# Two transformer layers on one core: later column sums in layer 1's projection stage, transposes moved in layer 0's expert loop

## The chip, the cores and the metric

The kernel runs on one core of a Trainium2 chip. The core has five engines that each work through their own queue in order: TensorE (PE in the profile, its weight loads PEld), VectorE (DVE), ScalarE (ACT), GpSimd (POOL) and SyncE (SP), which here only starts transfers. Engines wait for each other by semaphores. The metric is the device time of one execution in microseconds (us).

## The reference

Two layers work on 1024 latent tokens and 256 context tokens of width 1024. Layer 0 mixes by a short convolution and latent attention, layer 1 by windowed attention; each layer ends in a mixture of 16 experts in which each expert picks its tokens (128 latent and, in layer 0, 32 context tokens). What matters here:

```
aff = softmax(h @ router_w);  g, idx = top_k(aff.T, cap)       # every expert picks its tokens
xg  = h[idx]
hid = silu(xg @ w_gate) * (xg @ w_up)
out = zeros.at[idx].add((hid @ w_down) * g)
mod = silu(c) @ mod_w[layer] + mod_b[layer]                    # six rows of 1024: shift, scale, gate, twice
p   = modulate(rms_norm(x), shift, scale) @ w_qkv              # layer 1's projection, 10 tiles of 128 tokens
```

All arithmetic is float32. A large product is made of three matmuls on high and low parts: an operand is split by a cast on ACT (`wh`, `xh`, `hh`) and a subtraction on DVE (`wl`, `xl`, `hl`).

## The kernel before

**Layer 0's routing and its first expert.** `mixer_out` ends the mixer: it projects tiles of 128 tokens, and ranks the tokens for the experts. For the two context tiles, `OutTile.soft` (line 1290) makes the softmax of the router: two DVE operations, an exponential on ACT, a reciprocal and a product on DVE. Then `table(AF.Silu)` loads ACT's table for the experts. `moe` opens with `prep(0)`: the gathered tokens of expert 0 are transposed on PE and split into `xh` and `xl`; after that one piece of weights is converted, and `route_ctx` picks the context tokens.

**One expert of layer 0** (`expert`, line 1747). Its work on PE stands in program order (`manual_schedule` of PE and POOL); the order on ACT and DVE is laid down when the program is built, by a planner that runs the program in a model and gives each engine what is ready, the earlier in the program first. The order on PE is: `products(0, 0)` and `(0, 1)` (gate and up, first half of the columns), `ctx_products`, `products(1, 0)`, `turn(0)` and `ctx_turn(0)` (transposes of the hidden values, of latent and context tokens), `products(1, 1)`, `ctx_products`, `prep(e + 1)` (eight transposes of the next expert's tokens `xg`), after experts 3, 7 and 11 `prep_ctx` (eight transposes of the next four experts' context tokens `cx`), then the down products, steps `k` = 0 to 7 of six matmuls each, with `turn(1)` and `ctx_turn(1)` ahead of step 2, and last the context's down product `pcd`. All these transposes write the two PSUM buffers of tag B in turn, and a buffer is free again when ACT and DVE have read it: after `prep` that is the cast to `xh` and the subtraction to `xl`, after `ctx_turn` one ACT copy to `chT`. Steps 4 to 7 read `hh[1]` and `hl[1]`, which come from `turn(1)`. The weights have four buffers of `wh` and `wl`; each pair of down steps sets one free, and ACT then casts a piece of the next expert into it.

**Layer 1's projection** (`layer1_mixer`, line 1926) takes the ten tiles in turn, in program order on all queues. Between the products of the tiles it makes four of the six modulation rows that are needed later (`Row`, line 329): a row is four loads of 1 MB of `mod_w` by SP, four uses on DVE (each two multiply-adds of 128 x 1024 into an accumulator) and one `sum`: four small matmuls (`pm`) that add the accumulator over the partitions, one addition on DVE, one store by POOL. `modulations` (line 380) hands out these units one at a time, at most three in a tile, and loads `ahead` pieces ahead; here `ahead` is 1. All four rows share one accumulator, `lent`, borrowed from one of the rings of weight buffers. The sum follows its row's fourth use in the list, and PE takes it in program order between the tile's products.

Of the kernel before, what the change touches and what calls it, by code (L numbers as in the profile page):

```python
# [9 lines left out]
F32 = mybir.dt.float32  # L10
# [5 lines left out]
AF = mybir.ActivationFunctionType  # L16
# [5 lines left out]
D = 1024  # L22
# [14 lines left out]
ROWS_NEXT = [(1, r, (0,)) for r in (3, 4, 2, 5)]  # L37
E = 16
# [59 lines left out]
def hybrid_block_kernel(ctx, tc, A, out, dbg=None, upto=99):  # L98
# [42 lines left out]
    def table(f, src=ones):  # L141

        act.activation(warm, src, f, scale=0.0)

    rp = ctx.enter_context(sbuf("route"))
# [231 lines left out]
        def tile(self, shape, dtype, tag, **_):  # L377
            return self.tiles[tag]

    def modulations(parts, rows, ahead):  # L380

        a, b = [[u for x in xs for u in x.units()] for xs in (parts, rows)]
        todo = sorted([((i + 0.5) / len(x), i, u) for x in (a, b) for i, u in enumerate(x)], key=lambda t: t[0])
        todo = [u for _, _, u in todo]
        loads = [load for load, _ in todo if load]
        n = 0
        for load in loads[:ahead]:
            load()
        for load, use in todo:
            yield  # L390
            use()
            if load:
                n += 1
                for more in loads[n + ahead - 1:n + ahead]:
                    more()
# [793 lines left out]
    class OutTile:  # L1189
# [100 lines left out]
        def soft(self):  # L1290

            a = self.o.aff[self.s][:, self.i, :]
            m, d = [self.wp.tile([128, 1], F32, tag=t, bufs=2, name=t) for t in ("rm", "rd")]
            dve.scalar_tensor_tensor(a, self.lg, self.o.rr[self.s][:, self.i:self.i + 1], router[self.o.l, self.s][1],
                                     op0=ALU.mult, op1=ALU.add)
            dve.tensor_reduce(m, a, axis=AX.X, op=ALU.max, negate=True)
            act.activation(a, a, AF.Exp, bias=m, accum_out=d)
            dve.reciprocal(d, d)
            dve.tensor_scalar(a, a, d, None, op0=ALU.mult)

    def mixer_out(l, w_out, res_x, res_c, h2x_, acc_x_, routed, W):
        with sbuf("ow", side="right" if l else None) as wp, psum("owp", A=(4, 1), B=(2, 1), C=(2, 1)), tc.manual_schedule(engines=QUEUES):
# [161 lines left out]
            if l == 0:  # L1464
                W.convert(1)
                W.load(2)
                for y in tiles[8:]:
                    y.norm()
                o.scale(1)
                for y in tiles[8:]:  # L1470
                    y.mul()
                    y.add()
                    y.store()
                for y in tiles[8:]:
                    y.soft()
                routed[1] = o.aff[1]
                table(AF.Silu)
        if f"xm{l}" in dbg:
            if l == 0:
                pool.dma_start(dbg["xm0"][:NC], acc_c.rearrange("(t j) n -> t (j n)", j=4))  # L1480
# [212 lines left out]
    def moe(l, h2x_, acc_x_, routed, W, gates2, extra, last, early=None, then=None, finish=None, lent=[]):  # L1693
        gi, gv, xgs = {}, {}, {}
        XG, XH, HH, YO = CFG[l]
        with sbuf("moe") as mp, psum("mop", A=(4, 1), B=(2, 1), C=(2, 1)):
# [11 lines left out]
            def prep(e):  # L1708
                xg = xgs.pop(e)
                xh = mp.tile([128, 8, 128], F32R, tag="xh", bufs=XH, name="xh")  # L1710
                xl = mp.tile([128, 8, 128], F32R, tag="xl", bufs=XH, name="xl")
                for b, p in enumerate(transposes8(xg)):
                    bs = slice(b * 4, b * 4 + 4)
                    hilo(xh[:, bs, :], xl[:, bs, :], p.rearrange("p (k t) -> p k t", t=128))
                return xh, xl
# [7 lines left out]
            def prep_ctx(cx):  # L1723
                cT = mp.tile([128, 8, 128], F32, tag="cT", bufs=1, name="cT")
                for b, p in enumerate(transposes8(cx)):
                    act.copy(cT[:, b * 4:b * 4 + 4, :], p.rearrange("p (k t) -> p k t", t=128))
                return cT
# [8 lines left out]
            with tc.manual_schedule(engines=QUEUES):  # L1736
                look_up(0)
                gather(0)
                look_up(1)
                gather(1)  # L1740
                for e in range(2, 3 + 2 * l):
                    look_up(e)
                xT = prep(0)
                if l == 0:
                    W.convert(1)
                    cgi, cgv, cgg = route_ctx(mp, routed[1])
            def expert(e, xT, cT):

                look_up(e + (5 if l else 3))
# [33 lines left out]
                def turn(n):  # L1783

                    (p,) = transposes8(sil[n], 4)
                    hh.append(mp.tile([128, 4, 128], F32R, tag="hh", bufs=HH, name="hh"))
                    hl.append(mp.tile([128, 4, 128], F32R, tag="hl", bufs=HH, name="hl"))
                    hilo(hh[n], hl[n], p.rearrange("p (k t) -> p k t", t=128))
# [39 lines left out]
                    turn(1)  # L1828
                elif e:
                    ctx_products()  # L1830
                xT = prep(e + 1) if e + 1 < E else None
                if l == 0 and not e:
                    cT = prep_ctx(cx)
                    ctx_products()
                    ctx_turn(0)
                cT_ = cT
                if l == 0 and e % 4 == 3 and e + 1 < E:
                    cT_ = prep_ctx(cx)
                if e == E - 1:
                    if l == 0:  # L1840
                        turn(1)
# [5 lines left out]
                for k in range(8):  # L1847
                    if k % 2 == 0:
                        wd.append(W.get())
                    if k == 2 and l == 0:  # L1850
                        turn(1)
                        ctx_turn(1)
                    w = wd[k // 2]
                    for n in range(2):
                        ns = slice(n * 512, (n + 1) * 512)
                        pe.matmul(pd[n], hh[k // 4][:, k % 4], w[2][:, k % 2, ns], start=k == 0, stop=False)  # L1856
                        pe.matmul(pd[n], hh[k // 4][:, k % 4], w[1][:, k % 2, ns], start=False, stop=False)  # L1857
                    for n in range(2):
                        ns = slice(n * 512, (n + 1) * 512)
                        pe.matmul(pd[n], hl[k // 4][:, k % 4], w[1][:, k % 2, ns], start=False, stop=k == 7)  # L1860
# [65 lines left out]
    def layer1_mixer(st1, last, load_qkv, w_qkv, cols, x_first):  # L1926
        with sbuf("l1w") as wp, psum("l1p", A=(4, 1), B=(2, 1), C=(2, 1)):
# [118 lines left out]
            with tc.manual_schedule(engines=QUEUES):  # L2046
                x, y = tiles[:2]
                for z in tiles[:4]:
                    z.load()
                x.table()  # L2050
                w_hi(1)
                x.P()
                x.add()
                x.sq()
                y.P()
                w_hi(2)
                w_lo(dve)
                x.norm()
                w_lo(dve)
                while len(w_qkv) < 8:  # L2060
                    load_qkv()
                x.T()
                x.parts()
                w_hi(1)
                w_lo(dve)
                w_lo(pool)
                y.add()
                y.sq()
                w_hi(2)
                w_lo(dve)  # L2070
                w_lo(pool)
                y.norm()
                w_hi(2)
                w_lo(dve)
                w_lo(pool)
                lender = next(p for p, _ in ring.raws if p is not raw0)
                ring.less(lender)
                lent = Lent(lender.tile([128, 2, D], F32, tag="raw", bufs=2, name="lent"))
                rest = modulations([], [Row(l, r, ss, lent, "B") for l, r, ss in ROWS_NEXT], 1)
                for j in range(TT):  # L2080
                    x = tiles[j]
                    x1_, x2 = tiles[j + 1:j + 2], tiles[j + 2:j + 3]

                    def turn():
                        for y in x1_:
                            y.T()
                            y.parts()

                    for y in x1_:
                        y.table()  # L2090
                    for y in tiles[j + 4:j + 5]:
                        y.load()
                    if j == 0:
                        x.M(range(6), 2, 0, 1)
                        turn()
                        x.M(range(6, 8), 2, 0, 1)
                    for y in x2:
                        y.P()
                    if j not in (0, 1, 8):
                        turn()  # L2100
                    if j:
                        x.M(range(8), 2)
                        tiles[j - 1].q(1)
                    for y in x2:
                        y.add()
                        y.sq()
                        y.norm()
                    if j:
                        steps(rest, 1)
                    x.kv()  # L2110
                    if j > 1:
                        steps(rest, 1 if j < TT - 1 else 99)
                    if not x.s:
                        if j:
                            x.M(range(8), 0)
                        if j in (1, 8):
                            turn()
                        x.q(0)
                        if j:
                            steps(rest, 1)  # L2120
                            x.M(range(8), 1)
# [418 lines left out]
```

## Time and profile before

| | us |
|---|---|
| median of 3 runs | 2937.06 (2931.83 to 2937.67) |
| the profiled execution | 2937.01 |
| its span in the trace | 2935.2 |
| PE busy | 2693.3 (92%) |
| DVE busy | 2202.3 (75%) |
| ACT busy | 1618.6 (55%) |

A view of waits names who waited for whom, with total, times and longest. In a timeline a row is one instruction or several merged ones: start, duration, engine, line, operation, what it writes and reads, shapes, count, and in brackets how long the engine had been idle before it and what ended that. A view of windows gives the busy time of each engine in a stretch.

### The profile page before, as it was taken

Reading aid. Unit: us, or ns where it says so; the run is one execution under the profiler, and the core shown is the slowest. Engines: PE = TensorE matmul, PEld = TensorE weight load, DVE = VectorE, ACT = ScalarE, POOL = GpSimd, SP = SyncE. Lnnn points to the kernel's source line nnn. Section 1 sums busy time; section 2 is a strip of 40 time slices with the busy share of each in tenths; the row PEclk is TensorE's granted clock in tenths of the full one; section 3 lists DMA queues with packets and bytes.
Section 4 is the critical chain, followed back from the end, with each engine's and each line's share of the span. In section 5 each row is a group of like instructions: output and inputs, shape, how many; then the busy total and the mean of one; then the engine's idle time right before and its main releaser. Section 6 shows DMA issues by size and latency. Waiting matters only on the chain.

```text
span 2935.2 us, 43443 instructions
## 1 busy us (share of the span) xinstructions
PE 2693.3 (92%) x16939; PEld 2162.9 (74%) x16939; DVE 2202.3 (75%) x3425; ACT 1618.6 (55%) x2443; POOL 450.1 (15%) x294
## 2 busy tenths in 40 slices
PE   6999899999879999999999887799988599999996
PEld 5989899987657677677677665678867488877775
DVE  4775799986776666666666565799966688888886
ACT  4101578773245555555555532589943377776664
POOL 2100000000012110202111200232200522221103
PEclk8999999999989999999999998799999799999998
DMA  6552000027468787788787554311157699999993
GB/s 265 192 177 91 4 10 10 9 75 240 161 236 308 266 284 281 273 297 287 269 282 245 180 186 149 128 37 30 30 160 260 199 377 384 383 381 373 365 354 135
DMA packets 277198, 614.44 MB, mean 209 GB/s; under 512 B 25320, under 2 KB 73184, under 8 KB 274944
## 3 DMA queue, kind: packets, MB, share of 16 engines
q1 hardware_dynamic: 261840, 567.91, 53.8%
q0 software_dynamic: 15008, 43.62, 5.6%
q8 instruction: 133, 2.18, 0.3%
q14 instruction: 73, 0.60, 0.1%
q10 hardware_dynamic: 144, 0.13, 0.0%
HBM read 549.94 MB, written 61.67 MB: 208 GB/s over the span
## 4 chain that ended last, share of the span: by engine, by line
PE 68%; DVE 10%; ACT 4%; issue 4%; DMA 2%; POOL 1%; SPq 0%; DVEq 0%; ACTq 0%; POOLq 0%
PE pw L1223 6%; PE pg L1771 4%; PE pu L1773 4%; PE pu L1774 4%; PE pu L1776 4%; PE pg L1772 4%; PE pg L1775 4%; PE pd L1860 3%; PE pd L1856 3%; PE pd L1857 3%; PE po L979 3%; PE po L2267 2%; PE ppt L953 2%; PE pcg L1796 2%; PE ptr L407 2%
## 5 line engine op out<-in xcount | busy, mean ns | idle before, releaser
L1098 DVE TENSOR_TENSOR wl<-raw,wh 128x2048 fp32r<-128x2048 f32 x385 | 868.1, 2282 | 295.4 <-ACT wh L1097 295.4
L1097 ACT CAST wh<-raw 128x2048 fp32r<-128x2048 f32 (+1 forms) x392 | 733.8, 1902 | 336.8 <-PE pg L1775 218.8
L1865 POOL DMA_INDIRECT acc_x<-yo,gp x30 | 116.0, 3867 | 699.7 <-DVE yo L1864 658.8
L1771 PE MATMUL pg<-wl,xh 128*128 128x512 f32 x512 | 209.6, 409 | 4.5 <-ACT xh L164 4.5
L1773 PE MATMUL pu<-wl,xh 128*128 128x512 f32 x512 | 204.5, 399 | 6.0 <-DVE wl L1098 6.0
L1772 PE MATMUL pg<-wh,xh 128*128 128x512 f32 x512 | 203.8, 398 | 0.0
L1774 PE MATMUL pu<-wh,xh 128*128 128x512 f32 x512 | 203.1, 397 | 0.0
L1776 PE MATMUL pu<-wh,xl 128*128 128x512 f32 x512 | 203.1, 397 | 0.0
L1775 PE MATMUL pg<-wh,xl 128*128 128x512 f32 x512 | 203.0, 396 | 0.0
L1856 PE MATMUL pd<-wl,hh 128*128 128x512 f32 x480 | 195.6, 407 | 1.6 <-ACT csl L1802 1.6
L1857 PE MATMUL pd<-wh,hh 128*128 128x512 f32 x480 | 194.7, 406 | 0.0
L1860 PE MATMUL pd<-wh,hl 128*128 128x512 f32 x480 | 153.4, 401 | 1.0 <-DVE hl L165 1.0
L168 PE MATMUL pc<-hT,wh 128*128 128x256 f32 x480 | 140.2, 292 | 6.8 <-DVE h L481 5.0
L170 PE MATMUL pc<-hT,wl 128*128 128x256 f32 x480 | 137.6, 287 | 4.8 <-DVE wl L501 4.8
L169 PE MATMUL pc<-hT,wh 128*128 128x256 f32 x480 | 136.5, 284 | 0.0
L1771 PEld LDWEIGHTS pg<-wl,xh 128*128 128x128 f32 x512 | 96.7, 189 | 41.3 <-issue 17.1
L1773 PEld LDWEIGHTS pu<-wl,xh 128*128 128x128 f32 x512 | 96.6, 189 | 33.8 <-DVE wl L1098 11.5
L1780 ACT ACTIVATE sil<-pg 128x512 f32<-128x512 f32 x64 | 38.3, 598 | 143.8 <-PE pg L1775 143.8
L1796 PE MATMUL pcg<-raw,cT 128*32 128x256 f32 x2048 | 116.9, 381 | 0.1
L960 ACT CAST pt<-ppt 128x512 fp32r<-128x512 f32 (+1 forms) x192 | 95.0, 515 | 39.2 <-PE ppt L953 37.1
L964 DVE TENSOR_TENSOR pt<-ppt,pt 128x512 fp32r<-128x512 f32 (+1 forms) x192 | 110.6, 593 | 7.7 <-ACT pt L960 5.2
L1775 PEld LDWEIGHTS pg<-wh,xl 128*128 128x128 f32 x512 | 96.6, 189 | 23.2
(459 smaller groups left out, 6607.2 us busy)
## 6 DMA issues: line engine op xcount, KB each, us to landing
raw<-in_exp_w_gate_dram SPq DMA_DIRECT2D x128, 1024.0 KB
raw<-in_exp_w_up_dram SPq DMA_DIRECT2D x128, 1024.0 KB
raw<-in_exp_w_down_dram SPq DMA_DIRECT2D x128, 1024.0 KB
raw<-in_mod_w_dram SPq DMA_DIRECT2D x48, 1024.0 KB
yT<-yTd SPq DMA_DIRECT2D x17, 512.0 KB
acc_x<-xn SPq DMA_DIRECT2D x16, 512.0 KB
h2x<-h SPq DMA_DIRECT2D x16, 512.0 KB
raw<-in_w_in_dram SPq DMA_DIRECT2D x8, 768.0 KB
```

The lines of the kernel that those rows point to most:

```text
L1097: act.copy(wh[:, cs], raw[:, cs])
L1098: (eng or dve).tensor_sub(wl[:, cs], raw[:, cs], wh[:, cs].bitcast(F32))
L1223: pe.matmul(self.pp[n], a[:, k], b[k // 2][:, k % 2, ns], start=(k == 0 and i == 0), stop=(k == 7 and i == 2))
L1771: pe.matmul(pg, xh[:, k], gl[:, j], start=k == 0, stop=False)
L1772: pe.matmul(pg, xh[:, k], gh[:, j], start=False, stop=False)
L1773: pe.matmul(pu, xh[:, k], ul[:, j], start=k == 0, stop=False)
L1774: pe.matmul(pu, xh[:, k], uh[:, j], start=False, stop=False)
L1775: pe.matmul(pg, xl[:, k], gh[:, j], start=False, stop=k == 7)
L1776: pe.matmul(pu, xl[:, k], uh[:, j], start=False, stop=k == 7)
L1856: pe.matmul(pd[n], hh[k // 4][:, k % 4], w[2][:, k % 2, ns], start=k == 0, stop=False)
L1857: pe.matmul(pd[n], hh[k // 4][:, k % 4], w[1][:, k % 2, ns], start=False, stop=False)
L1860: pe.matmul(pd[n], hl[k // 4][:, k % 4], w[1][:, k % 2, ns], start=False, stop=k == 7)
```

## The change

Three edits. (1) `modulations` gets a parameter `late`: each sum is moved that many units down the list. Layer 1's rows are now loaded three pieces ahead, use two accumulators in turn, and are summed two units late. (2) The context tiles' softmax is cut in two: the two DVE operations stay in `mixer_out`, the exponential, the reciprocal, the product and the load of ACT's table are called in `moe` just before `route_ctx`, behind `prep(0)` and one conversion. (3) In layer 0's experts 1 to 14, `prep(e + 1)` moves from ahead of the down products to ahead of their step 4, `prep_ctx` to ahead of step 6, `ctx_turn(1)` to ahead of step 4, and `turn(1)` to ahead of step 0 (the two turns also in expert 0).

```diff
-    def modulations(parts, rows, ahead):
+    def modulations(parts, rows, ahead, late=0):
         a, b = [[u for x in xs for u in x.units()] for xs in (parts, rows)]
+        for i in reversed([i for i, (load, _) in enumerate(b) if not load] if late else []):
+            b.insert(i + late, b.pop(i))
...
-            m, d = [self.wp.tile([128, 1], F32, tag=t, bufs=2, name=t) for t in ("rm", "rd")]
+            m, d = [(rp if self.s else self.wp).tile([128, 1], F32, tag=t, bufs=2, name=t) for t in ("rm", "rd")]
...
+            self.s_ = a, m, d
+            if not self.s:
+                self.soft_rest()
+
+        def soft_rest(self):
+            a, m, d = self.s_
             act.activation(a, a, AF.Exp, bias=m, accum_out=d)
...
-                routed[1] = o.aff[1]
-                table(AF.Silu)
+
+                def soft():
+                    for y in tiles[8:]:
+                        y.soft_rest()
+                    table(AF.Silu)
+                    return o.aff[1]
+
+                routed[1] = soft
...
-                    cgi, cgv, cgg = route_ctx(mp, routed[1])
+                    cgi, cgv, cgg = route_ctx(mp, routed[1]())
...
-                xT = prep(e + 1) if e + 1 < E else None
+                xT = prep(e + 1) if (l or not e) and e + 1 < E else None
...
-                if l == 0 and e % 4 == 3 and e + 1 < E:
-                    cT_ = prep_ctx(cx)
...
-                    if k == 2 and l == 0:
+                    if l == 0 and k == 0:
                         turn(1)
+                    if l == 0 and k == 4:
                         ctx_turn(1)
+                        if e:
+                            xT = prep(e + 1)
+                    if l == 0 and k == 6 and e % 4 == 3:
+                        cT_ = prep_ctx(cx)
...
-                lent = Lent(lender.tile([128, 2, D], F32, tag="raw", bufs=2, name="lent"))
-                rest = modulations([], [Row(l, r, ss, lent, "B") for l, r, ss in ROWS_NEXT], 1)
+                lent = [Lent(lender.tile([128, 2, D], F32, tag="raw", bufs=2, name="lent")) for _ in range(2)]
+                rest = modulations([], [Row(l, r, ss, lent[i % 2], "B") for i, (l, r, ss) in enumerate(ROWS_NEXT)], 3, 2)
```

## Rows read from the trace of the kernel before

**Rows 1.** The page, part 1: busy time, share, instructions of each engine.
```profile
PE 2693.3 (92%) x16939; PEld 2162.9 (74%) x16939; DVE 2202.3 (75%) x3425; ACT 1618.6 (55%) x2443; POOL 450.1 (15%) x294
```

**Rows 2.** Windows: stretch, length, busy time of the engines, clock, DMA; layer 1's projection.
```profile
1700.00:1800.00 100.00, 81.62 (x345) 62.45 (x344) 65.53 (x127) 27.59 (x56) 2.80 (x5) 0.88 0.55 187
...
1694.20:1708.90 14.70, 13.80 (x64) 10.96 (x62) 12.42 (x24) 5.78 (x13) 0.54 (x1) 1.00 0.90 315
```

**Rows 3.** Waits of PE and of DVE, 1620 to 1845: total, times, longest.
```profile
PE pm L361 <- DVE lent L353: 27.8, 4, 9.5
...
DVE lent L353 <- DMA raw<-in_mod_w_dram: 12.9, 7, 3.9
```

**Rows 4.** Timeline of PE around the sums of layer 1's rows.
```profile
1743.72 1.92 PE L361 MATMUL pm<-lent,ones 128*32 128x512 f32 x4 [9.50 <-DVE lent L353]
1745.57 0.80 PE L168 MATMUL pqkv<-wl,hh 128*128 128x512 f32 x1
...
1749.98 0.39 PE L169 MATMUL pqkv<-wh,hh 128*128 128x512 f32 x1
1750.21 0.40 PE L170 MATMUL pqkv<-wh,hl 128*128 128x512 f32 x1
...
1822.07 1.92 PE L361 MATMUL pm<-lent,ones 128*32 128x512 f32 x4 [9.39 <-DVE lent L353]
```

**Rows 5.** Timeline of DVE: the last two uses ahead of the last sum.
```profile
1815.68 2.61 DVE L353 SCALAR_TENSOR_TENSOR lent<-raw,csil,lent 128x1024 f32<-128x1024 f32 x2 [3.28 <-DMA raw<-in_mod_w_dram]
1819.41 2.61 DVE L353 SCALAR_TENSOR_TENSOR lent<-raw,csil,lent 128x1024 f32<-128x1024 f32 x2 [1.13 <-DMA raw<-in_mod_w_dram]
```

**Rows 6.** Windows, one for each of experts 1 to 14, and their sum.
```profile
1126.09:1174.14 48.05, 47.75 (x360) 34.57 (x364) 33.09 (x24) 27.16 (x24) 6.98 (x4) 1.00 0.82 287
1174.14:1228.08 53.94, 50.50 (x368) 36.77 (x372) 33.09 (x24) 28.33 (x26) 9.89 (x5) 0.97 0.74 266
...
sum 691.57, PE 678.00 PEld 492.02 DVE 464.21 ACT 383.90 POOL 110.53; mean PE 48.43 PEld 35.14 DVE 33.16 ACT 27.42 POOL 7.90
```

**Rows 7.** Timeline of PE: an ordinary expert, then one with `prep_ctx`.
```profile
1266.66 0.66 PE L407 MATMUL ptr<-ident,sil 128*128 128x128 f32 x4 [0.30 <-DVE xl L165]
...
1406.63 1.09 PE L407 MATMUL ptr<-ident,xg 128*128 128x128 f32 x8
1410.81 1.25 PE L407 MATMUL ptr<-ident,cx 128*128 128x128 f32 x8 [3.08 <-DVE xl L165]
...
1414.36 0.63 PE L1856 MATMUL pd<-wl,hh 128*128 128x512 f32 x1
```

**Rows 8.** Timeline of ACT in two experts.
```profile
1362.50 1.90 ACT L1097 CAST wh<-raw 128x2048 fp32r<-128x2048 f32 x1 [1.71 <-PE pd L1860]
...
1364.78 0.27 ACT L1812 COPY chT<-pct 128x128 f32<-128x128 f32 x1
...
1407.50 0.38 ACT L1802 ACTIVATE csl<-pcg 64x256 f32<-64x256 f32 x1
```

**Rows 9.** Waits of PE's weight loads, 880 to 1590.
```profile
PEld pd L1860 <- DVE hl L165: 4.9, 14, 0.8
```

**Rows 10.** Timeline of PE after two short waits in expert 0.
```profile
840.10 0.50 PE L1773 MATMUL pu<-wl,xh 128*128 128x512 f32 x1 [1.37 <-DVE wl L1098]
...
865.48 0.50 PE L1856 MATMUL pd<-wl,hh 128*128 128x512 f32 x1 [1.59 <-ACT csl L1802]
...
867.45 0.63 PE L1857 MATMUL pd<-wh,hh 128*128 128x512 f32 x1
```

**Rows 11.** Timelines of PE and of ACT around `prep(0)`.
```profile
818.63 1.97 PE L407 MATMUL ptr<-ident,xg 128*128 128x128 f32 x8 [11.27 <-DMA xg<-h2x,gp]
825.14 0.76 PE L1771 MATMUL pg<-wl,xh 128*128 128x512 f32 x1 [4.54 <-ACT xh L164]
...
823.02 1.28 ACT L143 ACT_TABLE_LOAD   x1
...
824.43 1.05 ACT L164 CAST xh<-ptr 128x512 fp32r<-128x512 f32 x2
```

## The prediction

> **What bounds the kernel now.** I read the page first. Part 1 shows PE busy in 92% of the span [rows 1], so a gain has to come out of PE's remaining 8%, or out of stretches in which PE runs at the lower of its two clock levels. The windows then say where that is: in the hundred microseconds of layer 1's projection PE is busy 81.62 at a mean granted clock of 0.88 [rows 2], while an ordinary expert of layer 0 has PE busy 47.75 of 48.05 at full clock [rows 6]. The waits of PE name the cause in the projection: one group, the small matmuls `pm` behind DVE's accumulation, 27.8 us in four waits [rows 3]. In the experts the reader is to see that three of the fourteen last 53.94 or a little more instead of 48.05 [rows 6], and in the timeline what is in them: a wait of 3.08 for `xl` ahead of the transposes of `cx` [rows 7]. Ahead of expert 0 PE stands for 4.54 because `xh` comes late [rows 11]. These are the three places that the change touches.
>
> **Part 1, layer 1's rows.** Before: PE meets a sum in program order and waits until DVE has made the row's fourth use. DVE is late for two reasons: it waited 12.9 us for pieces of `mod_w` that were loaded only one ahead [rows 3], and it is nearly full, 12.42 of 14.70 us in a tile with three uses [rows 2]. Afterwards PE goes on at half pace: behind the wait of 9.50 the ten matmuls from 1745.57 to 1749.98 take 4.41, where the pace is 0.23 each (1749.98 to 1750.21), so 2.1 too long, and `pm` takes 1.92 where an undisturbed one has about 1.05 by the same factor; together 2.9 [rows 4]. [...]
>
> After: in the list of units (four uses and a sum for each row) sums 1 to 3 stand two uses later, which is most of a tile (72 products of 0.23, some 17 us), against a longest wait of 9.5. They find their accumulators ready, and the second buffer lets the next row start without them. The loads are three ahead, and there are three buffers, so a load now waits on SP for the use that frees its buffer; behind it in SP's queue stand stores that wait for later DVE work anyway, so that costs nothing. POOL's stores of the rows move with the sums; the tile loads queued behind them are needed more than a tile later. The number of uses, sums, loads and stores stays.
>
> The fourth sum can't move: the list ends behind it, so it still follows its use directly. Of its wait of 9.39 [rows 4] the two waits for transfers, 3.28 and 1.13, go [rows 5], and one use of 2.5 goes too, since a sum takes the place of a use in the tile before. 2.5 stays, plus a slow stretch behind it.
>
> Sum: 27.8 - 2.5 = 25.3 of waits, plus the slow stretches behind the second and third wait, 2.9 and (a shorter wait) about 2: 30 us. What is late next is DVE: three uses in a tile take 84% of PE's time as shown, so tiles with a sum and two uses have room. Bounds: 34 if even the last wait goes with its clock; 24 if DVE lags by its 2 us of slack at each of the four sums.
>
> **Part 2, the context softmax.** Before, the eight transposes end at 820.60 and the cast to `xh` begins at 824.43, because ACT has two exponentials and the table load (1.28, from 823.02) first [rows 11]. After, the casts come first: the first half is transposed by about 819.6, so `xh` is there near 820.2 instead of 825.0, and PE could start 4.5 sooner. The same 3 us of ACT work now stand between the third and the fourth conversion of weights, so the second pair of weights may be late by 1 to 1.5, inside what was gained. The context's exponentials move from before 823.0 to about 824 (the casts to 821.2, a conversion of 1.9), and the list that hangs on them is needed only when expert 0's four products are through, over 20 us later. I take 3.5 less. Bounds: 4.5 (the whole wait), and 1.5 more than before (the fourth conversion late and nothing gained, because the gather of the context's tokens ends the first expert's wait).
>
> **Part 3, the experts.** Fourteen experts take 691.57 [rows 6]. What goes: the 0.30 ahead of `turn(1)` [rows 7] in eleven of them, 3.3; the waits of the down products for `hl`, 4.9 over all [rows 9], since `turn(1)` now comes four steps (5.5 us) ahead of its first reader; and in the three long ones the 3.08 and the slow stretch behind it. Such an expert is 53.94 - 48.05 = 5.89 longer; 1.0 of it are the transposes of `cx` (1410.81 to the next), 2.78 the longer wait, the remaining 2.1 the lower clock (0.63 where 0.39 is usual, until past 1414.36 [rows 7]). So 3 x (3.08 + 2.1) = 15.5. Sum 23.7.
>
> What comes: (a) The down products start about 0.3 sooner after `ctx_products`, because a `turn` is half as long as `prep`; their second PSUM buffer is free only when ACT has made `csl`, at 1407.88 where the products now would want it at 1407.6 [rows 7, 8]: 0.25 each, 3.5 in all.
>
> (b) A new wait. The second half of `prep` needs the buffer that `ctx_turn(1)` has just filled, so PE waits for ACT's copy to `chT`. Step 3 has just set weight buffers free at that moment, and ACT is idle. The rows show what ACT's fixed order makes of this one place earlier: as soon as a down step releases a buffer it starts the cast (1362.50), and `chT`, ready a moment later, follows behind it (1364.78) [rows 8]. So I expect the cast first: 1.81 until the next instruction, and 0.27 for `chT`, 2.15 with the signals, while PE has only six of eight transposes' worth of work (about 0.7 of the 0.85 that eight take). The wait is 1.45, fourteen times: 20.3. Queued behind it on PE are all the rest of the expert; nothing hides it. From below it costs 0 (the copy goes ahead of the cast), from above two casts, 3.3.
>
> (c) `prep_ctx` at step 6 needs the buffers of `prep`, read by two casts of 0.5 [rows 11] and two subtractions like them, in the 2.8 us of steps 4 and 5: ready just in time, 0. The next expert's `xh` and `xl` have steps 4 to 7, 5.5 us, and `pcd`: 0. `xh` no longer waits for the last product.
>
> Sum: -23.7 + 3.5 + 20.3 = 0. The three long experts lose what the eleven others pay. Bounds: 20 less (no new wait), and more than before if the clock falls (rivals).
>
> Whether a wait of 1.45 lowers the clock: the rows have both. After 1.37 the next matmul is at full pace, after 1.59 matmuls take 0.63 [rows 10]; after 3.08 they did all three times [rows 7]. I take no fall, as after the row nearest to 1.45. [...]
>
> **Sum.** 2937.0 (the profiled execution, span 2935.2 and 1.8 around it; the median of the runs is 2937.06, the same) - 30 - 3.5 + 0 = 2903.
>
> **Rivals.**
> A. No new wait in the experts: `chT` is put ahead of the cast. For it: of things ready together ACT takes the earlier in the program, and `chT` is that. Against it: [rows 8]. 2903 - 20 = 2883.
> B. The clock falls after each of the fourteen new waits, at the price seen after 3.08, 2.1 each, 29 in all: 2932. For it: [rows 10], 1.59. Against it: 1.37 in the same rows.
> C. The change doesn't do in layer 1 what it says: the sums find another wait, since DVE's own work, not the loads, made it late. Half of the 30 comes back: 2918. Against it: two units' distance is more than any wait.
> D. Slower: in the experts the clock, once lowered at step 4, stays so through the rest of the down products. 24 matmuls at 0.43 instead of 0.23 are 4.8; fourteen times 67, so 2970. It decides from 34 / 14 = 2.4 us lost behind each wait, only a little above B's 2.1. Against it: after the 3.08 the slow stretch cost 2.1, not 4.8.
>
> **Chances.** Forecast 0.50, A 0.22, B 0.10, C 0.12, D 0.06. The time is the forecast's. The range 2880 to 2930 holds the forecast with the bounds of parts 1 and 2, A, C, and half of B; outside are D and B's upper half. A measurement of this kernel can tell about 0.2% (6 us) from no change: faster 0.89 (forecast, A, C, half of B), same 0.05 (the other half), slower 0.06 (D).
>
> **What would show it.** Part 1: waits of PE for `lent` fall from 27.8 to a few us in one wait, and the projection's clock stands near 1. Part 2: the cast to `xh` ahead of the table load. Part 3: in ordinary experts a wait ahead of `prep`'s second four transposes, released by `chT`, and windows near 49 us; in A they are near 47.7; in B the clock is below 1 in all of them. Wrong it would be if the ordinary experts lasted over 51, or if `pm` still waited for 10 us or more.

## The result, and the profile after

The changed kernel takes 2898.95 us (median of 4 runs, 2897.56 to 2900.43), the kernel before beside it 2934.56. The ratio is 0.9878, with a 95% interval of 0.9861 to 0.9896, so 30 to 41 us less; the forecast was 2903. One execution of a later kernel, turn_at_3_shift, took 5315 us where its five others took 2888, and its ratio leaves that one out. The profiled execution took 2898.11, its span 2896.3, which is 38.9 less than the span of before.

Layer 1's projection first. The windows, in the columns of [rows 2], are 100 us in the middle of it:

```profile
1664.00:1764.00 100.00, 98.40 (x449) 78.36 (x448) 77.83 (x160) 39.72 (x82) 3.31 (x6) 1.00 0.73 253
```

PE is busy 98.40 of 100 at a clock of 1.00, where [rows 2] had 81.62 at 0.88. The waits of PE have one line left of the four waits in [rows 3]:

```profile
PE pm L361 <- DVE lent L353: 2.0, 1, 2.0
```

The timeline of PE shows the first and the last of the four sums (the second, at 1740.88, and the third, at 1778.06, look like the first); they answer to [rows 4]:

```profile
1707.45 1.05 PE L361 MATMUL pm<-lent,ones 128*32 128x512 f32 x4
...
1786.88 1.05 PE L361 MATMUL pm<-lent,ones 128*32 128x512 f32 x4 [2.02 <-DVE lent L353]
1787.87 0.50 PE L168 MATMUL pqkv<-wl,hh 128*128 128x512 f32 x1
```

All four take 1.05, none 1.92: the granted clock is 1.00 at each of them. Only the last waits, 2.02, and the products behind it are at full pace.

Ahead of expert 0, PE and then ACT, to be read against [rows 11]:

```profile
816.39 1.97 PE L410 MATMUL ptr<-ident,xg 128*128 128x128 f32 x8 [11.34 <-DMA xg<-h2x,gp]
818.27 0.77 PE L1786 MATMUL pg<-wl,xh 128*128 128x512 f32 x1
...
827.07 0.51 PE L1788 MATMUL pu<-wl,xh 128*128 128x512 f32 x1 [1.21 <-DVE wl L1101]
...
840.72 0.24 PE L1547 MATMUL pidx<-ident,cidf 16*32 16x16 f32 x5 [2.49 <-DVE cidf L1540]
```

```profile
817.54 0.59 ACT L164 CAST xh<-ptr 128x512 fp32r<-128x512 f32 x1 [15.49 <-PE ptr L410]
...
820.69 0.31 ACT L1306 ACTIVATE raff<-raff,rm 128x16 f32<-128x16 f32 x1
...
821.39 1.28 ACT L143 ACT_TABLE_LOAD   x1
```

The casts to `xh` come first now and the first product follows the transposes at once; the wait of 4.54 is gone, and 1.21 for the second pair of weights stands in its place. The 1.37 for weights of [rows 10] is gone too, but PE now waits 2.49 for `cidf`, the list of context tokens that hangs on the moved softmax. In the kernel before PE came to that list without a wait:

```profile
844.72 0.26 PE L1532 MATMUL pidx<-ident,cidf 16*32 16x16 f32 x7
```

The experts in windows (an ordinary one, one with `prep_ctx`, the sum of fourteen), then the new wait on PE and on ACT; they answer to [rows 6 to 8]:

```profile
1119.87:1169.05 49.18, 47.69 (x358) 34.59 (x357) 33.12 (x24) 27.27 (x24) 6.97 (x4) 1.00 0.80 281
1169.05:1219.09 50.04, 48.58 (x366) 35.44 (x365) 33.98 (x24) 28.25 (x26) 9.87 (x5) 1.00 0.81 287
...
sum 691.19, PE 670.46 PEld 486.92 DVE 464.56 ACT 384.94 POOL 108.84; mean PE 47.89 PEld 34.78 DVE 33.18 ACT 27.50 POOL 7.77
```

```profile
1155.30 0.50 PE L1874 MATMUL pd<-wl,hh 128*128 128x512 f32 x1 [0.18 <-ACT csl L1817]
...
1160.90 0.66 PE L410 MATMUL ptr<-ident,xg 128*128 128x128 f32 x4
1162.86 0.65 PE L410 MATMUL ptr<-ident,xg 128*128 128x128 f32 x4 [1.31 <-ACT chT L1827]
1163.27 0.48 PE L1874 MATMUL pd<-wl,hh 128*128 128x512 f32 x1
```

```profile
1160.74 1.91 ACT L1100 CAST wh<-raw 128x2048 fp32r<-128x2048 f32 x1 [0.89 <-PE pd L1878]
1162.55 0.26 ACT L1827 COPY chT<-pct 128x128 f32<-128x128 f32 x1
```

The cast is ahead of the copy to `chT`, PE waits 1.31 for it, and the clock stays at 1.00 in all fourteen. The long experts are shorter by 3.9 us (the first by 4.9), the ordinary ones longer by 1.1, and the sum is what it was. The waits of PE from 860 to 1600 put it in one line:

```profile
PE ptr L410 <- ACT chT L1827: 18.2, 14, 1.3
```

So far the forecast holds. But the terms measured in this profile (30.4 in the projection, 3.5 ahead of expert 0, 0.4 in the experts) leave 4.6 of the 38.9 over: 2.2 ahead of `prep(0)` and 2.4 behind the projection. Both are within what executions of like code differ by: copies_3 and copies_of_chT below, which are the kernel after in both places, reach `prep(0)` at 819.0 and 816.5 (after 816.4, before 818.6) and take 1086.7 and 1088.9 behind the projection (after 1089.5, before 1091.9). And whether a term comes from the edit that it was put down to, one pair of profiles can't say.

### The profile page after: what moved, and what is told of

Read it like the earlier page. It is cut to its first block, busy times and chain, and to the rows that moved or that the text cites. A ratio compares the mean times of both kernels' runs of the same rounds, so it can differ in the third digit from the quotient of the medians.

```text
span 2896.3 us, 43462 instructions
## 1 busy us (share of the span) xinstructions
PE 2677.9 (92%) x16939; PEld 2152.5 (74%) x16939; DVE 2200.8 (76%) x3425; ACT 1620.5 (56%) x2443; POOL 449.8 (16%) x294
## 4 chain that ended last, share of the span: by engine, by line
PE 71%; DVE 7%; ACT 6%; issue 2%; DMA 1%; POOL 1%; SPq 0%; DVEq 0%; ACTq 0%; POOLq 0%
PE pw L1226 6%; PE pg L1786 4%; PE pu L1788 4%; PE pu L1789 4%; PE pu L1791 4%; PE pd L1878 4%; PE pd L1874 4%; PE pg L1790 4%; PE pg L1787 4%; PE pd L1875 4%; ACT wh L1100 3%; PE po L982 3%; PE po L2285 2%; PE ppt L956 2%; PE ptr L410 2%
```

## The experiments

All were timed in five rounds beside the kernel before (median 2935.85 to 2937.04 in the three groups; the kernel after as above). Stages of each profiled execution, us: from the transposes of `prep(0)` to expert 0's first `pcd`; the fourteen experts; from there to the load of `ks` that ends the projection; what follows up to the end. The 816 to 821 us ahead of `prep(0)` are not in the table.

| kernel | median | ratio (95%) | prep(0) | experts | projection | behind it |
|---|---|---|---|---|---|---|
| before | 2937 | 1 | 60.1 | 691.6 | 273.0 | 1091.9 |
| after | 2899.0 | 0.9878 (0.9861 to 0.9896) | 56.6 | 691.2 | 242.6 | 1089.5 |
| rows_only | 2904.4 | 0.9881 (0.9866 to 0.9896) | 60.4 | 691.6 | 244.2 | 1093.1 |
| loads_only | 2927.8 | 0.9972 (0.9962 to 0.9982) | 60.3 | 691.5 | 265.5 | 1089.3 |
| late_only | 2915.9 | 0.9930 (0.9913 to 0.9947) | 60.2 | 691.7 | 252.3 | 1092.4 |
| soft_only | 2928.8 | 0.9966 (0.9954 to 0.9979) | 57.1 | 688.2 | 277.0 | 1086.1 |
| shift_128 | 2926.1 | 0.9965 (0.9954 to 0.9975) | 59.2 | 684.3 | 274.1 | 1087.1 |
| experts_only | 2937.8 | 0.9998 (0.9989 to 1.0007) | 60.1 | 693.7 | 276.3 | 1091.2 |
| no_soft | 2907.4 | 0.9902 (0.9887 to 0.9916) | 58.8 | 693.7 | 245.9 | 1088.9 |
| no_soft_shift | 2903.9 | 0.9892 (0.9877 to 0.9906) | 59.8 | 691.2 | 242.4 | 1089.5 |
| turn_at_3 | 2882.2 | 0.9811 (0.9795 to 0.9826) | 56.8 | 675.8 | 241.2 | 1089.5 |
| turn_at_3_shift | 2888.2 | 0.9838 (0.9825 to 0.9850) | 56.8 | 678.3 | 243.1 | 1089.5 |
| copies_3 | 2898.7 | 0.9874 (0.9857 to 0.9891) | 56.6 | 691.2 | 242.7 | 1086.7 |
| copies_of_chT | 2969.0 | 1.0114 (1.0100 to 1.0129) | 56.6 | 762.9 | 242.9 | 1088.9 |

### Layer 1's rows: all of edit 1, its loads, its place

rows_only is the kernel before with edit 1 as it stands; the other two take it apart:

```diff
 rows_only:   Row(..., lent[i % 2], "B") ..., ahead 3, late 2
 loads_only:  Row(..., lent[i % 2], "B") ..., ahead 3, late 0
 late_only:   Row(..., lent[i % 2], "B") ..., ahead 1, late 2
```

> The kernel before with edit 1 alone (layer 1's rows). Theory (the three parts add up, and part 1 is 30 us of PE waiting for sums and of the lower clock behind them): 30 us less than before, some 2905; PE waits for `lent` once, about 2 us, ahead of the last sum; the projection's stretch is some 30 shorter, everything ahead of it is as before. Rival (part of those 30 us is had only because the stretches ahead were changed too, so that the pieces of `mod_w` come at other moments): 15 to 20 less, with a second wait for `lent` of several us.

> The kernel before with two parts of edit 1 (two buffers of sums, pieces of `mod_w` loaded three ahead), but each sum straight behind its row's last use, as before. Theory (the waits of PE for `lent` are in part DVE waiting for pieces, 12.9 of the 27.8 before, in part DVE's own work, which the later place of the sums hides): the waits for `lent` fall from 27.8 to some 15, and with what goes of the slow stretches the kernel takes 12 to 16 us less than before, some 2923. Rival (the loads were all of it, the later place is worth nothing): 30 less, as with all of edit 1. Other rival (the place is all of it): no change.

> The kernel before with the other parts of edit 1 (two buffers of sums, each sum two uses later), but pieces loaded one ahead, as before. Theory: sums 1 to 3 are hidden whatever the loads do, since two uses of distance are some 17 us; the last keeps DVE's waits for pieces, some 7 to 9 us: 22 to 26 us less than before, some 2913. Rival (DVE falls behind by more than the distance when it waits for pieces): two or more waits for `lent`, 10 to 15 less.

Measured: 33, 9 and 21 us less than before by the medians. In rows_only PE waits for `lent` as in the kernel after, once, 2.0. Its waits in loads_only, and in late_only, there with DVE's for pieces:

```profile
PE pm L361 <- DVE lent L353: 19.1, 3, 7.9
```

```profile
PE pm L361 <- DVE lent L353: 8.9, 1, 8.9
...
DVE lent L353 <- DMA raw<-in_mod_w_dram: 9.3, 4, 4.2
```

Edit 1 gives its gain by itself, with the one wait of 2.0 that it has in the kernel after: the rival that it needs the other edits is out. With the loads three ahead DVE no longer waits for pieces in this stretch, and PE still waits 19.1: the loads were worth 8.7 of the 27.8, less than the expected 12 or so. The later place is worth more: even with DVE waiting 9.3 for pieces (and 3.1 more ahead of a row's first use), the first three sums are hidden, and the last keeps 8.9. Neither part is all of it. In the projection's stage the two give 7.5 and 20.7, together 28.2, and all of edit 1 gives 28.8, so they add up. Both kernels have the second buffer of sums; what it is worth alone no run shows.

### The experts: edit 3 alone, and its new wait taken out

experts_only is the kernel before with edit 3 as it stands. turn_at_3 is the kernel after with one line moved:

```diff
+                    if l == 0 and k == 3:
+                        ctx_turn(1)
                     if l == 0 and k == 4:
-                        ctx_turn(1)
                         if e:
                             xT = prep(e + 1)
```

> The kernel before with edit 3 alone (transposes placed elsewhere among the down products). Theory (what the three long experts lose the eleven others pay): the time of before within 3 us; ordinary experts 49.2 instead of 48.05, long ones 50.05 instead of 53.9; fourteen waits of 1.3 for `chT`, clock 1.00. Rival (the edit gains by itself, and the equal sum of the two profiles is chance): 10 us less or more.

> The kernel after with the transposes of the second half of `csl` (ctx_turn(1)) one step earlier, ahead of the conversion that step 4 asks for; nothing else. Theory (the new wait is `chT` queued on ACT behind that conversion, 1.30 in each of fourteen experts): the wait goes, ordinary experts last 47.9 instead of 49.2, and the kernel takes 18 us less than after, some 2881. Rival (the two halves of `prep` find another wait, for the copy itself or for the buffer of turn(1)): within 6 us of after, 2893 to 2905, with a wait of a like size under another name.

Edit 3 alone makes no difference, 0.9998. In its windows an ordinary expert, a long one and the sum:

```profile
1127.46:1176.79 49.33, 47.84 (x358) 34.59 (x357) 33.11 (x24) 27.27 (x24) 6.99 (x4) 1.00 0.80 280
1176.79:1227.03 50.24, 48.74 (x365) 35.44 (x365) 33.98 (x24) 28.26 (x26) 9.90 (x5) 1.00 0.78 286
...
sum 693.67, PE 672.76 PEld 487.16 DVE 464.53 ACT 384.99 POOL 108.95; mean PE 48.05 PEld 34.80 DVE 33.18 ACT 27.50 POOL 7.78
```

By itself it costs 2.1 in the experts (693.67 against 691.57). And an ordinary expert is some 0.2 longer than in the kernel after, where it is the same code; more on that below. One gain of the forecast is missing here. The waits of the weight loads for `hl`, 4.9 in all [rows 9], are gone, but PE's products had run on beside them. In the kernel before, with such a wait of 0.24 inside, the last 36 down products of an ordinary expert take 8.56, and in experts_only, without it, the last 24 take 5.69, from the first of them to `pcd`:

```profile
1165.51 0.51 PE L1856 MATMUL pd<-wl,hh 128*128 128x512 f32 x1
...
1174.07 2.15 PE L1873 MATMUL pcd<-raw,chT 128*32 128x256 f32 x36
```

```profile
1171.10 0.48 PE L1859 MATMUL pd<-wl,hh 128*128 128x512 f32 x1
...
1176.79 0.64 PE L1876 MATMUL pcd<-raw,chT 128*32 128x256 f32 x8
```

That is 0.238 and 0.237 a product, where a wait that cost PE its 0.24 would have made it 0.244.

turn_at_3 is the fastest of all, 17 us under after by the medians, 15.4 of it in the experts' stage. PE and ACT in an expert of it:

```profile
1155.01 0.33 PE L1826 MATMUL pct<-ident,csl 64*128 64x64 f32 x2
1156.78 1.04 PE L410 MATMUL ptr<-ident,xg 128*128 128x128 f32 x8
```

```profile
1153.72 1.91 ACT L1100 CAST wh<-raw 128x2048 fp32r<-128x2048 f32 x1 [2.22 <-PE pd L1879]
1155.53 0.25 ACT L1827 COPY chT<-pct 128x128 f32<-128x128 f32 x1
```

The copy still stands behind a cast, though an earlier one. What has changed is that PE has a step of down products to do meanwhile, and `prep` runs through its eight transposes without a wait. So the wait was the price of edit 3, as the forecast had it. The three long experts now wait 1.2 each for `xl` ahead of `cx` and last 50.2, the ordinary ones 47.7.

### The context softmax, and what came with it

soft_only is the kernel before with edit 2 as it stands.

> The kernel before with edit 2 alone (the context softmax behind the casts to xh). Theory: 3.5 us less, some 2931; expert 0's first product without a wait behind the eight transposes instead of 4.54, and one wait of about 1.2 for the second pair of weights instead. Rival (the 3.5 seen between the two profiles is drift of the transfer that ends the wait for xg): same within 1 us, and the first product still starts several us after the transposes.

It took 8 us less, more than twice the forecast of its term. Ahead of expert 0 it gave 3.0 of that, with the first product straight behind the transposes as forecast, so the rival of a drifting transfer is out. But the experts were 3.4 shorter, and edit 2 changes nothing in them; the projection was 4.0 longer and what is behind it 5.8 shorter, for no cause that these runs show. One thing of it reaches everywhere: it takes four small tiles (`rm` and `rd`, 32 bytes each as laid out) from the pool `rp` that stays, and so moves all SBUF tiles that are allocated later from the left by 128 bytes. shift_128 does that alone, and turn_at_3_shift does it once more on top of turn_at_3:

```diff
     rp = ctx.enter_context(sbuf("route"))
+    rp.tile([128, 32], F32, name="gap")
```

> The kernel before with nothing but 128 unused bytes more in each SBUF partition, ahead of all that is allocated from the left: exactly the addresses that edit 2 gives, which puts four small tiles there. With edit 2 alone the kernel took some 8 us less, 3 of them ahead of expert 0; ordinary experts last 47.82 instead of 48.05, though edit 2 changes nothing in them. Theory (the addresses set the pace of the expert products: 24 of them with their stops take 5.40 instead of 5.47): experts of 47.82 here too, and some 5 us less than before, 2932. Rival (it is the moved exponentials, the order of ACT's work or chance): experts of 48.05 and the time of before within 1.5 us.

> The kernel of turn_at_3 with 128 unused bytes more, so all that is allocated from the left lies 256 bytes higher than in the kernel before. Theory (what decides repeats every 256 bytes, and the addresses of before were the worse ones): the 24 expert products take 5.47 again, ordinary experts 47.95 instead of 47.72, 5 to 10 us more than turn_at_3, some 2889. Rival (it was the distance to one neighbour, and stays gone): 5.40, 47.72 and the time of turn_at_3, 2882.

shift_128 took 11 us less than before by the medians, as much as edit 2 and twice what was expected, without any work moved. The first and the twenty-fourth product of one half of an expert, in the kernel before and then in shift_128:

```profile
1081.57 0.50 PE L1771 MATMUL pg<-wl,xh 128*128 128x512 f32 x1
...
1087.04 0.39 PE L1776 MATMUL pu<-wh,xl 128*128 128x512 f32 x1
```

```profile
1076.55 0.51 PE L1772 MATMUL pg<-wl,xh 128*128 128x512 f32 x1
...
1081.94 0.39 PE L1777 MATMUL pu<-wh,xl 128*128 128x512 f32 x1
```

From start to start that is 5.47 and 5.39, the same instructions at the same granted clock, 1.00. In windows, three of its experts:

```profile
972.94:1025.12 52.18, 48.80 (x365) 35.58 (x365) 33.10 (x24) 28.34 (x26) 9.87 (x5) 1.00 0.79 275
...
1120.77:1168.60 47.83, 47.58 (x358) 34.59 (x357) 33.10 (x24) 27.16 (x24) 6.98 (x4) 1.00 0.82 289
1168.60:1222.28 53.68, 50.30 (x366) 36.77 (x365) 33.09 (x24) 28.33 (x26) 9.87 (x5) 0.97 0.76 267
```

The ordinary one takes 47.83 instead of 48.05. (Two of the three long ones are at 1.00, about 1.5 shorter than the third: after their wait of 3.1 the clock stayed up. That, not the addresses alone, is why this run's experts have 684.25. In soft_only, at these addresses and with the same waits, the clock of all three is at 0.97 or 0.94.) turn_at_3_shift goes the other way, as expected:

```profile
1117.60:1165.48 47.88, 47.70 (x357) 34.59 (x356) 33.10 (x24) 27.15 (x24) 6.97 (x4) 1.00 0.82 289
```

The same two products in it:

```profile
1073.30 0.50 PE L1787 MATMUL pg<-wl,xh 128*128 128x512 f32 x1
...
1078.76 0.40 PE L1792 MATMUL pu<-wh,xl 128*128 128x512 f32 x1
```

That is 5.46 again, at 256 bytes. Against turn_at_3 its ordinary experts are 0.16 longer, the sum 2.5, the median 6 us. So with 128 bytes the gate and up products are faster (5.39 for 5.47), and with 256 that is given back (5.46). That it repeats every 256 bytes was the author's estimate: the runs have these three places and no other. The down products go the other way: the last 24 take 5.69 in experts_only (1171.10 to 1176.79 above) and 5.78 in the kernel after (1163.27 to 1169.05, in the rows of the result). It is no scatter: the 96 gate and up products of an ordinary expert take 22.88 to 22.90 in the seven kernels at the addresses of before or 256 bytes on, and 22.53 to 22.56 in the seven that are 128 bytes on. Which pair of tiles does it, and by what, these runs don't show.

That leaves the question how much edit 2 did itself. no_soft is the kernel after without edit 2, and no_soft_shift the same with the gap of 128 bytes.

> Edits 1 and 3 together, without edit 2, at the addresses of before. It asks how much of edit 2 in the kernel after is its own work and how much is the 128 bytes by which it shifts all that is allocated from the left (alone these gave 10 us in the kernel before). Theory (both): ordinary experts 49.35 as with edit 3 alone, the wait of 4.5 for `xh` ahead of expert 0 back, and some 8 us more than after: 3 from expert 0's start, 2.5 from the experts, 2 to 3 from the rest; some 2907. Rival (the edits add up as they did alone, 35 and -0.6): 2902.

> As no_soft, with the 128 unused bytes of the earlier run, so at the addresses of the kernel after, but with the softmax where it was. What this takes more than after is edit 2's own work. Theory: ordinary experts 49.17, the wait of 4.5 for `xh` still there, 2 to 3.5 us more than after, 2902. Rival (the shift is worth something only beside the old order of transposes): experts of 49.35 and the same time as no_soft.

They took 2907.4 and 2903.9: 8.4 and 4.9 more than after. At the addresses of after the experts are what they are there to a hundredth, 691.19, at the others 693.68; and the wait that edit 2 takes away is back in no_soft_shift:

```profile
PE pg L1774 <- ACT xh L165: 4.4, 1, 4.4
```

In the stage of `prep(0)` it is 59.8 against 56.6, so 3.2 from moving the softmax. The other pair at equal addresses, shift_128 and soft_only, has 59.2 against 57.1, so 2.1; there the whole time shows no gain (2926.1 and 2928.8), with two of shift_128's long experts 1.5 shorter by the clock. The intervals of no_soft and no_soft_shift overlap, so the medians don't settle how edit 2's gain is divided between its own work and the addresses; the stages do, for `prep(0)` and for the experts.

### Longer waits in the experts, and the clock

Two kernels lengthen the new wait of the kernel after. The first failed: its copies had nothing to wait for.

```diff
 copies_3, in ctx_turn:       for _ in range(3): act.copy(sil[0], sil[0])
 copies_of_chT, in ctx_turn:  for _ in range(9): act.copy(chT[...], p[...])     # once in the kernel after
```

> The kernel after with three useless copies (`sil[0]` onto itself, 0.6 us each) on ACT ahead of the copy to `chT`, in each of the fourteen experts: the wait of PE behind the first half of `prep` grows from 1.30 to some 3.1. It tells how long a wait must be here to lower the clock. Theory (a wait of 1.3 left the clock at full, waits of 3.1 lowered it in the kernel before, at 2.1 us each): 14 x (1.8 + 2.1) = 55 us more than after, some 2954; granted clock in the experts below 1, matmuls of 0.63 behind the wait. Rival (the clock fell in the kernel before for another reason than the length of the wait): 14 x 1.8 = 25 more, some 2924, clock 1.00.

> The kernel after with the copy to `chT` made nine times instead of once in each of the fourteen experts; since each of them reads the new transposes, none of them can run ahead of these. The wait of PE behind the first half of `prep` grows from 1.30 to some 3. Theory (a wait of 1.3 left the clock at full, waits of 3.1 lowered it in the kernel before, at about 2 us each): 14 x (1.7 + 2.1), 53 us more than after, some 2952; matmuls of 0.63 behind the wait. Rival (the clock fell there for another reason than the length of the wait): 14 x 1.7, 24 more, some 2923, the matmuls behind the wait at 0.39.

copies_3 took 2898.74, the time of after. ACT's order is laid down by the planner, which put the copies where `sil[0]` was ready, in a gap of ACT 14 us earlier, and the wait stayed 1.30:

```profile
1150.81 1.95 ACT L1826 COPY sil<-sil 128x512 f32<-128x512 f32 x3
...
1165.56 0.66 PE L410 MATMUL ptr<-ident,xg 128*128 128x128 f32 x4 [1.30 <-ACT chT L1829]
```

It shows only that 1.95 of ACT's time in each expert costs nothing there. copies_of_chT took 2969.04, ratio 1.0114 (1.0100 to 1.0129), 70 more than after. PE in one expert of it, and the window of the slow stretch:

```profile
1190.27 1.11 PE L410 MATMUL ptr<-ident,xg 128*128 128x128 f32 x4 [4.04 <-ACT chT L1828]
...
1191.61 0.63 PE L1876 MATMUL pd<-wh,hh 128*128 128x512 f32 x1
...
1196.13 0.39 PE L1875 MATMUL pd<-wl,hh 128*128 128x512 f32 x1
```

```profile
1190.00:1196.00 6.00, 5.73 (x16) 4.67 (x17) 0.94 (x2) 0.80 (x2) 0.00 (x0) 0.51 0.01 4
```

The wait became 4.04, longer than the 3 that was meant. Behind it everything runs at about half pace (0.63 a matmul where 0.39 is usual, granted 0.51 in this window) until 1196.13. An ordinary expert takes 54.4 instead of 49.18: 2.7 of these 5.2 are the longer wait, 2.5 the clock. The theory's mechanism is what the rows show; its 53 us were too few because the wait came out a microsecond longer and the clock cost 2.5 a time instead of 2.1.

## Why the prediction was right

**Part 1, -30.** Right in mechanism and size. The projection's stage is 273.0 to 277.0 in the four kernels without edit 1, and 241.2 to 245.9 in the eight with all of it: 32 by the means. The last sum kept 2.0 where 2.5 was forecast, and the first three wait for nothing. The forecast let a slow stretch stand behind the last sum; in the kernel after none follows, but in rows_only and no_soft one does, behind the same wait. The distance was overstated: only the third sum moved by 72 products, the first by 24 and the second by 48 (the products of the projection ahead of each sum, counted in both traces). It was enough, since each of the three finds its accumulator ready 6 us or more before. Rival C said that DVE's own work, not the loads, made the sums late. On that point it was right: with the loads mended 19.1 of waits remain. It fell on its consequence, since two uses of distance cover this work too.

**Part 2, -3.5.** Right in size: 3.2 and 2.1 at equal addresses, with the late second pair of weights (1.21) inside, as forecast. In part that is luck. The list of context tokens was forecast to be in time, and PE waits 2.49 for it; in return the 1.37 for weights went, and PE's waits behind `prep(0)` for `xl` and for `csl` fell from 1.55 and 1.59 to 0.96 and 1.24. The edit brought 128 bytes along that the prediction didn't see: some 2.5 us in the experts of the kernel after (693.68 to 691.19). In the projection no_soft takes 3.5 more than no_soft_shift, but 1.6 of that is a slow stretch behind its last sum, and such stages differ by as much from run to run.

**Part 3, 0.** Right in its mechanism, and the sum is met by two misses that cancel. The long experts lost their 3.08 with the clock behind it. The new wait is 1.30 fourteen times, 18.2 for the forecast 20.3, with the cast ahead of the copy; `csl` costs 0.18 an expert where 0.25 was put. What failed is the term of 4.9 for `hl`: those were waits of weight loads. In an ordinary expert (0.24) products run beside them and almost nothing came of it; in a long one (0.77) PE stands still for a part of it, but that lies inside the 5.89 that the forecast had already taken apart, so it was counted twice. So edit 3 by itself costs 2.1 in the experts where 0 was forecast, and the 0.4 gained in the kernel after is the 2.5 of the addresses less these 2.1. Of the 2.1 put down to the clock in a long expert, 1.5 is the clock: in shift_128 the one that lost it lasts 53.68, the two that kept it 52.18 and 52.16. Rival A needed the copy ahead of the cast, which ACT's order didn't give; turn_at_3 shows that its price was right, 17 us by the medians for a forecast 20.

**The clock.** Rivals B and D fell: after 1.30 the next down product takes 0.48 and its successors 0.39, as the forecast had it from the row of 1.37 [rows 10]. At waits of 1.30, one in each 49 us, the clock is 1.00 in all fourteen experts of the kernel after; behind waits of 4.04, in copies_of_chT, it falls in all fourteen. The two levels of the forecast are those of the traces: the granted clock before and after is 1.00 or 0.50 in every stretch (before, 0.50 from 1745 to 1749, behind the wait of 9.50, and 1.00 from 1750.2 to 1754). D's point of decision, 2.4 lost behind each wait, is about what copies_of_chT loses to the clock, and that kernel, which loses another 2.7 to each longer wait, is slower than before. Between the two the rows differ. Ahead of `cx`, waits of 3.08 to 3.10 lowered the clock in sixteen of eighteen long experts (before, rows_only, loads_only, late_only, soft_only, shift_128), and the two others are in shift_128. Ahead of the last sum, waits of 2.02 to 2.04 left it up in six of the eight kernels with all of edit 1 and lowered it in rows_only and no_soft. In no_soft it looks like this, to be read against 1786.88 of the kernel after:

```profile
1798.00 1.62 PE L361 MATMUL pm<-lent,ones 128*32 128x512 f32 x4 [2.03 <-DVE lent L353]
...
1800.14 0.63 PE L169 MATMUL pqkv<-wh,hh 128*128 128x512 f32 x1
```

The forecast took its "no fall" from one row. That it held is shown, fourteen times in each of the five kernels that have the wait of 1.30 (after, experts_only, no_soft, no_soft_shift, copies_3); that one row was enough to tell it is luck.

**The sum.** 2903 forecast, 2899 measured. The runs show three things that the forecast didn't have, the shift by 128 bytes (2.5 less in the experts), the missing gain for `hl` and the wait for the context's list, and they pull in both directions. With medians that move by 2 to 3 us, the 4 us between forecast and result can't be put down to any of them.

## What to carry to other kernels

Give an accumulator a second buffer and its reader a place further down the list, before loading further ahead: here the place gave 21 us and the loads 9, each with the second buffer. When a transpose is moved to save a long wait, look at which engine must empty the PSUM buffer, and what that engine has queued ahead; one step between the filling and the next use of the buffer was worth 17 us. Before counting a wait of PE's weight loads, look whether the products run on beside it: here 0.24 in each ordinary expert was worth almost nothing. And where an edit allocates from a pool that lives long, time the allocation alone too: a gain of 0.2 to 0.35% came with the addresses here.

## What had not been expected of the hardware

In these runs a shift of 128 bytes in SBUF changed the pace of the same matmuls at the same granted clock, 1.00: 24 products of 512 columns took 5.39 (shift_128) instead of 5.47 us (before) from the first start to the last, and with a further 128 bytes 5.46 (turn_at_3_shift), while the down products went the other way (24 of them 5.78 in the kernel after instead of 5.69 in experts_only). Over the kernel that was 11 us in the one pair and 6 in the other; the pace of the experts' products is 3.4 (by soft_only) and 2.5 of it, the clock in shift_128's long experts some 4 more (684.3 against soft_only's 688.2), and the rest was not traced.

A wait of 3.1 us in the same place of the same loop lowered the clock sixteen times of eighteen, and one of 2.0 us ahead of the last sum twice in eight kernels, so the length alone doesn't decide there.
